# Moving a 30-column copy to ScalarE, merging four scans, and taking a rate ahead of a product, in a stick-breaking attention and convolution layer

## Chip, cores and metric

The kernel runs on one core of one Trainium2 chip. The metric is the device time of one execution in microseconds. The engines of the core are TensorE (PE in the profile, with its weight loads as PEld), VectorE (DVE), ScalarE (ACT), GpSimd (POOL) and SyncE (SP, which here only issues DMA transfers).

## The reference

One layer of a streaming encoder over 2048 tokens of width 1024, with 16 learned meta tokens in front. All arithmetic is in float32.

```python
u = rms_norm(h, pre_g)
glu_a, glu_b, conv_gate, q, k, v, sb_gate = split(u @ w_in)      # 7 x 512 columns

c = glu_a * sigmoid(glu_b)
c = causal_depthwise_conv(c, conv_w, conv_b)                     # 31 taps
c = silu(layer_norm(c)); c = (c @ w_pw2 + b_pw2) * silu(conv_gate)

# stick-breaking attention, 8 heads of 64: with z = q.k / 8 and s < t
# A[t,s] = sigmoid(z[t,s]) * prod over s < j < t of (1 - sigmoid(z[t,j]))
s = (A @ v) * silu(sb_gate)

mixed = concat([c, s]) @ w_out
out = (h + rms_norm(mixed, post_g))[16:]
```

## The kernel before, in words

**Number format.** Every float32 product is made of three products of a faster format: a value is split into a high part (a copy, by ScalarE) and a low part (the value less its high part, by VectorE or GpSimd). In the profile the names `uh` and `ul`, `ah` and `al`, and pairs called `w`, `mixs` or `mixc` are such parts.

**Chunks.** The tokens go through in four chunks of 512 (`c` = 0 to 3), each in four blocks of 128. Activations lie transposed, channels on the partitions. A chunk passes through these steps:

- *Projection*, `in_proj`: products of `uh`, `ul` with streamed weights into PSUM banks `mm`. `pairs` makes the gated convolution input: from the bank of `glu_b` ScalarE takes a sigmoid, and VectorE multiplies the bank of `glu_a` by it into `ct[j]`, one buffer for each of four groups of 128 channels (`j` = 0 to 3). `ct[j]` has 30 columns of history (`HIST`) ahead of the chunk's 512. For every chunk but the first, the last 30 columns of the chunk before are copied to the front of the buffer first: 12 copies in all (3 chunks, 4 groups). The product then overwrites the columns that the copy has read.
- *Convolution*: `conv` runs 31 taps on VectorE with the running sum in a PSUM bank `cv`; for some groups `conv_apart` makes each product on ScalarE (`pd`) and adds it on GpSimd (`acc`).
- *Attention*: for each head and key chunk, `weigh` makes logits in a PSUM bank `T`, ScalarE takes a sigmoid, and a scan on VectorE (`pr`) makes the running products. `flip` turns them on TensorE in another bank `T`, and splits the result: ScalarE writes `ah`, VectorE writes `al`, and the bank is free then. `gather` multiplies by the values (`vk`) into the bank `av`. There are four banks of `T`.
- *Meta tokens*, `meta_keys`: the same scan goes on over the 16 meta keys. `sgm` holds for each block and head 17 numbers, 16 sigmoids and a zero; `cm` holds zeros and, at the 17th place, the product that the head's scan ended with. Since `sgm` is zero there, the scan `max(state * sgm, cm)` starts afresh from that number at each head. For chunks 0, 1 and 2 all heads go together (`part` is false); for the last chunk they go in smaller parts.
- *Output*: `out_proj`, and for the last chunk `out_part` and `out_last`, with the norm over the mixed channels.

**Order.** One core's five engines each run their own list in order. The lists are written when the program is built, by a planner: `Clock` and `Engine` hold a model of what every instruction costs on its engine and when its inputs are there; `merge` picks, step by step, the next group of products of the attention stream (`main`), of the projections and the convolution (`fill`) and of the meta tokens (`extra`), and `step` issues the work of the other engines that is due by the model's clock of TensorE. Taps of the convolution are put into VectorE's gaps. So an instruction that is given to another engine changes the modelled clocks of both, and what is placed behind it can change with them. The code of the end, `out_last`, is written out by hand.

**The end.** The last chunk's last 256 columns are made last. `square` takes the sum of their squares on ScalarE (`accum_out`), VectorE multiplies them by the post-norm weights (`pg`), `rate` sums the partial sums on VectorE and takes the power -1/2 on GpSimd (`st`), and `give_out` multiplies by the rate, adds the input, on VectorE, and stores.

**The start.** `warm` issues transposes of the identity on TensorE while the first transfers are under way.

Every instruction is issued through one helper, so most rows of the profile name its line, L228; tiles and shapes tell the rows apart.

Of the kernel before, what the change touches and what calls it, by code (L numbers as in the profile page):

```python
# [14 lines left out]
AF = mybir.ActivationFunctionType  # L15
# [9 lines left out]
TC = 512  # L25
NCH = SEQ // TC
NTB = TC // P
# [5 lines left out]
HIST = CW - 1  # L33
# [243 lines left out]
def trunk(ctx: ExitStack, tc: tile.TileContext, x, xturn, xlater, meta, cpack, post_g, wpack, out):  # L277
# [20 lines left out]
    dve = Engine(clock, nc.vector, dve_cost, 0.04, run)  # L298
    act = Engine(clock, nc.scalar, act_cost, 0.04, run)
# [32 lines left out]
    def PT(tag, shape):  # L332
        bufs = BANKS[tag]
        room(tag, bufs)
        t = ps.tile(shape, F32, tag=tag, name=tag, bufs=bufs)
        clock.take(tag, bufs, t.name)
        return t
# [58 lines left out]
    ct = [const.tile([P, HIST + TC], F32, name=f"ct{j}") for j in range(NJ)]  # L396
# [151 lines left out]
    there = set()  # L548
# [226 lines left out]
    def warm():  # L775


        pt = PT("T", [P, TC])
        for _ in range(17):
            pe.transpose(pt[:, :P], ident, ident)  # L780

    waiting = []
# [8 lines left out]
    def tok():  # L791
        return T("tok", [P, 2, D], 2)
# [162 lines left out]
    def pairs(c, js):  # L955
        base = HIST - NM
        for j in js:
            sgb = []

            def ev_b(pt, o, n, j=j, sgb=sgb):  # L960
                if not sgb:
                    sgb.append(T("ehl", [P, NM + TC], EHL))
                t = sgb[0][:, o : o + n]

                def go():
                    dve.tensor_tensor(t, pt, row[:, o : o + n], op=ALU.mult)
                    act.activation(t, t, AF.Sigmoid)
                    if j < EARLY_PAIRS:

                        pool.tensor_tensor(t, t, row[:, o : o + n], op=ALU.mult)  # L970

                if c == 0 and j < EARLY_PAIRS:
                    with_rates(go)
                else:
                    act.activation(t, pt, AF.Sigmoid)

            def ev_a(pt, o, n, j=j, sgb=sgb):
                t, to = sgb[0][:, o : o + n], ct[j][:, base + o : base + o + n]

                def go():  # L980
                    dve.tensor_tensor(to, pt, t, op=ALU.mult)
                    if o + n < NM + TC:
                        return
                    if c and c - 1 not in parted:
                        parted_later.append(conv(c, j))
                    elif j in APART[c]:
                        taps_apart.append(conv_apart(c, j))
                    else:
                        taps.append(conv(c, j))

                if c == 0:
                    with_rates(go)
                else:
                    dve.tensor_copy(ct[j][:, 0:HIST], ct[j][:, TC : TC + HIST])
                    go()

            yield from proj(c, G_B + j, ev_b, True)
            if j < BEFORE[c]:
                yield need(given=lambda: j in accs[c - 1])
            yield from proj(c, G_A + j, ev_a, True)  # L1000
# [498 lines left out]
    def meta_keys(c, h0, h1, mixs):  # L1499

        hs = slice(h0, h1)
        part = h1 - h0 < NH
        yield need(
            given=lambda: all(("total", c, h) in keep for h in range(h1))
            and (c < NCH - 1 or ("conv" if h0 else "room", c) in keep)
        )
        for j in range(NJ):
            force(f"v{j}")
        bm = ev()[:, :TC].rearrange("p (b h s) -> p b h s", b=NTB, h=NH)
        hold.add(bm.name)  # L1510
        if part:
            pool.memset(bm, 0.0)
        sgm = sgms[c % 2]
        zm = sgm[:, :, hs, 0:NM]
        for r in range(NTB):
            fl = lambda t: t[:, r, hs].rearrange("p h s -> p (h s)")[:, ::-1]
            dve.tensor_tensor_scan(
                fl(sgm), fl(sgm), fl(cm), 0.0, op0=ALU.mult, op1=ALU.max
            )
        when(lambda: pool.tensor_copy(bm[:, :, hs], zm), [sgm], [bm])  # L1520
        given = {}
        force("s")
        force("g")

        def bring(j):
            sp.dma_start(given[j][1], sscr[c, j])
            sp.dma_start(given[j][0], gscr[c, j])
            when(lambda: rest(j), [given[j][1], vcol[c % 2]], [given[j][1]])

        def rest(j):  # L1530
            sr = given[j][1]
            s4 = sr.rearrange("p (b t) -> p b t", t=P)
            pool.tensor_tensor(
                s4, s4, vcol[c % 2][:, j].unsqueeze(2).to_broadcast([P, NTB, P]), op=ALU.add
            )

        def fetch(j):
            if j:
                given[j] = [ev()[:, :TC] for _ in range(2)]
                hold.update(t.name for t in given[j])  # L1540
            else:
                given[j] = keep["first given"]
            bring(j)

        js = range(h0 // 2, h1 // 2)
        if not part:
            both = [tok().rearrange("p j (i t) -> p j i t", i=2) for _ in range(2)]
            for j in js:
                given[j] = [both[j // 2][:, j % 2, i] for i in range(2)]
                in_us(0.8 * j, lambda j=j: bring(j), outs=[given[j][1]])  # L1550
        else:
            fetch(js[0])
        yield need(bm, tag="T", given=None if part else room_for_turned)
        hold.remove(bm.name)
        pt = PT("T", [P, TC])
        for r in range(NTB):
            pe.transpose(
                pt[:, r * P : (r + 1) * P], bm[:, r].rearrange("p h s -> p (h s)"), ident
            )
        high, low = slice(2 * NM, 4 * NM), slice(0, 2 * NM)  # L1560
        meets = {}
        turned = pt if part else T("ehl", [P, TC], EHL)
        if not part:
            act.activation(turned, pt, AF.Copy)
        for j in js:
            src = turned[2 * j * NM : 2 * (j + 1) * NM]
            m = meets[j] = T(*(("ehl", [P, TC], EHL) if part else ("mixs", [P, TC], 8)), F32R)
            hold.add(m.name)
            act.activation(m[high], src, AF.Copy)
            dve.tensor_tensor(m[low], src, m[high].bitcast(F32), op=ALU.subtract)  # L1570
            pool.tensor_copy(m[4 * NM : 6 * NM], m[high].bitcast(F32))
        if part:
            yield need(given=lambda: ("conv", c) in keep)
        for j in js:
            if j + 1 in js and j + 1 not in given:
                fetch(j + 1)
            gt, sr = given[j]
            m = meets[j]
            ready, t0 = need(m, vm, sr, gt, tag="T"), pe.now + 1.8
            yield lambda: ready() if part else max(ready(), t0)  # L1580
            pj = PT("T", [P, TC])
            pe.matmul(pj, vm[: 6 * NM, j], m[: 6 * NM], start=True, stop=True)
            hold.difference_update((sr.name, gt.name, m.name))
            dve.tensor_tensor(pj if part else sr, pj, sr, op=ALU.add)
            (dve if part else pool).tensor_tensor(sr, pj if part else sr, gt, op=ALU.mult)
            hi = T("mixs", [P, TC], 8, F32R)
            lo = T("mixs", [P, TC], 8, F32R)
            split(sr, hi, lo)
            mixs[j] = hi, lo
# [84 lines left out]
    def out_last(y, mh, ml):  # L1674
# [24 lines left out]
        def square(tb, src, n):  # L1699
            junk = T("ev", [P, TC], EV, BF16)[:, : src.shape[1]]  # L1700

            act.activation(
                junk, src, AF.Square, scale=D ** -0.5, accum_out=sums[:, tb, n : n + 1]
            )

        def place(tb, h):
            return y[tb // 2][:, tb % 2, h * TC : (h + 1) * TC]
# [5 lines left out]
            square(tb, a, 0)  # L1713
            dve.tensor_tensor(yt, a, pg[:, 0], op=ALU.mult)

        def add_second(tb, e=None, there=False):
            cols = slice(0, TC) if e is None else slice(e * OC, (e + 1) * OC)
            o = keep["o", tb, e or 0][:, cols]
            keep["end", tb, 1] = o if there else place(tb, 1)
            square(tb, o, 1 + (e or 0))  # L1720
            dve.tensor_tensor(o if there else place(tb, 1)[:, cols], o, pg[:, 1, cols], op=ALU.mult)

        def rate(tb):
            ss, rates[tb] = T("ss", [P, 1], 2), T("st2", [P, 1], 8)
            dve.tensor_reduce(ss, sums[:, tb], axis=mybir.AxisListType.X, op=ALU.add)
            pool.tensor_tensor(rates[tb], ss, nhalf, op=ALU.pow)
# [49 lines left out]
        finish_off(rest)  # L1776
        second(3, 1)
        give_out(2)
        add_second(3, 1)
        rate(3)  # L1780
        give_out(3)

    def out_proj(c, mixc, mixs):
# [262 lines left out]
```

## Time and profile before

| | |
|---|---|
| three runs | 1300.95, 1301.02, 1302.16 us (median 1301.02) |
| the profiled execution | 1302.12 us, of which its span from the first to the last instruction 1300.3 us |
| mean granted clock of TensorE | 0.997 |
| history copies on VectorE (128x30) | 12, together 8.6 us |
| meta scans on VectorE (128x136) | 12, together 7.4 us |
| warming transposes | 17, from 1.82 us on, 3.7 us |
| last product of TensorE begins at | 1293.5 us |

A row of a timeline has the start in us from the span's start, the duration, the engine, the helper's line, the operation, output and inputs (`ct<-mm,ehl` writes `ct` from `mm` and `ehl`), shapes, and how many instructions are merged in it; in brackets stands the time that the engine was idle before it and whose work ended that. A row of groups has the count, then the busy time in us and the mean in ns. A row of windows has the stretch, its length, the busy time of PE, PEld, DVE, ACT and POOL, the granted clock, the share of the DMA engines and GB/s.

### The profile page before, as it was taken

The numbers are of one execution on the slowest core, as the hardware profiler recorded it, in microseconds if no ns is written. First come the engines' busy times: TensorE is split into PE (matmuls) and PEld (weight loads), VectorE is DVE, ScalarE is ACT, GpSimd is POOL, SyncE is SP. The second block draws the span as 40 slices with busy tenths as digits, with TensorE's granted clock in tenths as the row PEclk, the third lists the DMA queues.
The fourth block names the chain that finished last, engine by engine and source line by source line (L and its number), as shares of the span: only waits on it lengthen the run. The fifth ranks groups of instructions, "written<-read, shape, count | busy, mean of one in ns | idle before, by whom it ended". The sixth has DMA issues, their size and how long they took to land. (4 is left out here: it accounts for less than half of the span.)

```text
span 1300.3 us, 22358 instructions
## 1 busy us (share of the span) xinstructions
PE 1280.6 (98%) x7458; PEld 1108.8 (85%) x7458; DVE 1022.3 (79%) x1426; ACT 792.1 (61%) x1666; POOL 694.5 (53%) x819
## 2 busy tenths in 40 slices
PE   8999998999999999999999999999999999999998
PEld 8998877888889988888889988888887899988897
DVE  5999898888986488984477569895558888898974
ACT  6544455444556555687755446688887865665653
POOL 2556567767687631586982242287788812132402
PEclk9999998999999999999999999999999999999999
DMA  6687875687977996676866697657667556587745
GB/s 241 217 266 250 271 234 178 211 249 239 291 242 245 311 327 188 193 241 200 283 209 181 176 313 239 177 169 231 215 207 228 158 150 188 172 263 235 232 138 182
DMA packets 177731, 290.57 MB, mean 223 GB/s; under 512 B 20928, under 2 KB 75392, under 8 KB 177616
## 3 DMA queue, kind: packets, MB, share of 16 engines
q1 hardware_dynamic: 166384, 251.65, 62.5%
q0 software_dynamic: 11232, 37.49, 7.6%
q8 instruction: 59, 0.97, 0.3%
q14 instruction: 56, 0.46, 0.1%
HBM read 222.10 MB, written 66.98 MB: 222 GB/s over the span
## 5 line engine op out<-in xcount | busy, mean ns | idle before, releaser
L228 PE MATMUL mm<-uh,w 128*128 128x512 f32 (+1 forms) x1936 | 562.5, 376 | 1.4 <-ACT uh L228 1.4
L228 PEld LDWEIGHTS mm<-uh,w 128*128 128x128 f32 x1936 | 337.5, 188 | 53.1 <-ACT uh L228 1.9
L228 PE MATMUL mm<-ul,w 128*128 128x512 f32 (+1 forms) x968 | 357.7, 371 | 1.3 <-DVE ul L228 1.3
L228 DVE TENSOR_TENSOR_SCAN pr<-T,pr,zcol 128x512 f32<-128x512 f32 x192 | 245.0, 1277 | 42.2 <-ACT T L228 40.4
L228 DVE TENSOR_TENSOR al<-T,ah 128x512 fp32r<-128x512 f32 (+1 forms) x320 | 192.1, 601 | 103.2 <-ACT ah L228 101.4
L228 ACT ACTIVATE ah<-T 128x512 fp32r<-128x512 f32 (+1 forms) x320 | 169.7, 530 | 127.5 <-PE T L228 126.3
L228 DVE SCALAR_TENSOR_TENSOR cv<-ct,cp,cv 128x512 f32<-128x512 f32 x319 | 239.1, 750 | 6.7
L228 POOL TENSOR_TENSOR acc<-acc,pd 128x512 f32<-128x512 f32 x150 | 193.7, 1291 | 56.4 <-ACT pd L228 50.2
L228 PEld LDWEIGHTS mm<-ul,w 128*128 128x128 f32 x968 | 181.7, 188 | 35.4 <-DVE ul L228 2.5
L228 POOL TENSOR_TENSOR w<-wr,w 128x512 fp32r<-128x512 f32 x132 | 171.0, 1298 | 74.9 <-ACT w L228 62.4
L228 PE MATMUL T<-kk,q 128*128 128x512 f32 (+4 forms) x704 | 201.2, 374 | 5.5 <-DVE al L228 4.9
L228 ACT ACTIVATE T<-T 128x512 f32<-128x512 f32 (+2 forms) x320 | 167.0, 523 | 50.2 <-PE T L228 43.5
L228 ACT ACTIVATE w<-wr 128x512 fp32r<-128x512 f32 x220 | 138.0, 628 | 95.9 <-PE mm L228 57.6
L228 PE MATMUL T<-ident,pr 128*128 128x128 f32 x1088 | 171.1, 272 | 0.6 <-DVE al L228 0.6
L228 PEld LDWEIGHTS T<-ident,pr 128*128 128x128 f32 x1088 | 133.9, 140 | 29.8 <-DVE al L228 1.0
L228 DVE TENSOR_TENSOR_SCAN pr<-T,tri 128x128 f32<-128x128 f32 (+3 forms) x128 | 104.3, 818 | 37.4 <-ACT T L228 33.9
L228 PEld LDWEIGHTS T<-kk,q 128*128 128x128 f32 x704 | 115.2, 190 | 21.0 <-DVE al L228 5.8
L228 PE MATMUL av<-al,vk 128*128 128x512 f32 (+1 forms) x320 | 117.2, 366 | 0.0
L228 PE MATMUL av<-ah,vk 128*128 128x512 f32 (+1 forms) x320 | 117.0, 366 | 0.0
L228 ACT ACTIVATE pd<-ct,cp 128x512 f32<-128x512 f32 x150 | 105.3, 714 | 1.4 <-POOL acc L228 1.2
L228 POOL COPY cm<-pr 128x1 f32<-128x1 f32 x120 | 24.8, 208 | 130.9 <-DVE pr L228 128.6
L228 PE MATMUL mm<-w,mixc 128*128 128x256 f32 x600 | 81.2, 284 | 0.0
(207 smaller groups left out, 1584.4 us busy)
## 6 DMA issues: line engine op xcount, KB each, us to landing
wr<-wpack SPq DMA_DIRECT2D x220, 256.0 KB, 3.8
w<-wscr SPq DMA_DIRECT2D x70, 512.0 KB, 4.6
vk<-vscr SPq DMA_DIRECT2D x80, 256.0 KB, 3.5
w<-lscr SPq DMA_DIRECT2D x80, 256.0 KB, 2.8
kk<-kscr SPq DMA_DIRECT2D x72, 256.0 KB, 4.3
q<-qscr SPq DMA_DIRECT2D x64, 256.0 KB, 5.3
wscr<-w POOLq DMA_DIRECT2D x28, 512.0 KB, 4.3
lscr<-w POOLq DMA_DIRECT2D x40, 256.0 KB, 3.5
```

The lines of the kernel that those rows point to most:

```text
L228: return call(out, *args, **kw)
```

## The change

Four edits. The history copy in `pairs` becomes an activation (plain copy) on ScalarE. In `meta_keys`, where all heads go together, one scan over all four blocks, 544 columns, replaces four of 136; in the last chunk's parts the four scans stay. In `out_last`, for the very last columns the rate is asked for between the square and the product: VectorE's sum comes ahead of its product, and GpSimd's power follows that sum. `warm` issues 22 transposes in place of 17.

```diff
         pt = PT("T", [P, TC])
-        for _ in range(17):
+        for _ in range(22):
             pe.transpose(pt[:, :P], ident, ident)
...
                 else:
-                    dve.tensor_copy(ct[j][:, 0:HIST], ct[j][:, TC : TC + HIST])
+                    act.activation(ct[j][:, 0:HIST], ct[j][:, TC : TC + HIST], AF.Copy)
                     go()
...
-        for r in range(NTB):
-            fl = lambda t: t[:, r, hs].rearrange("p h s -> p (h s)")[:, ::-1]
+        for rs in [slice(r, r + 1) for r in range(NTB)] if part else [slice(0, NTB)]:
+            fl = lambda t: (
+                t[:, rs.start, hs].rearrange("p h s -> p (h s)")
+                if part
+                else t.rearrange("p b h s -> p (b h s)")
+            )[:, ::-1]
             dve.tensor_tensor_scan(
                 fl(sgm), fl(sgm), fl(cm), 0.0, op0=ALU.mult, op1=ALU.max
             )
...
-        def add_second(tb, e=None, there=False):
+        def add_second(tb, e=None, there=False, rated=False):
             cols = slice(0, TC) if e is None else slice(e * OC, (e + 1) * OC)
             o = keep["o", tb, e or 0][:, cols]
             keep["end", tb, 1] = o if there else place(tb, 1)
             square(tb, o, 1 + (e or 0))
+            if rated:
+                rate(tb)
             dve.tensor_tensor(o if there else place(tb, 1)[:, cols], o, pg[:, 1, cols], op=ALU.mult)
...
         give_out(2)
-        add_second(3, 1)
-        rate(3)
+        add_second(3, 1, rated=True)
         give_out(3)
```

## The prediction

> **What bounds the kernel now.** I read the page first, for the busy shares and the granted clock.
>
> ```profile
> span 1300.3 us, 22358 instructions
> PE 1280.6 (98%) x7458; PEld 1108.8 (85%) x7458; DVE 1022.3 (79%) x1426; ACT 792.1 (61%) x1666; POOL 694.5 (53%) x819
> PEclk9999998999999999999999999999999999999999
> ```
>
> TensorE is busy for 1280.6 of 1300.3 us, and the diff removes no product of it. So all that can be won is the 19.7 us in which it is idle, and time in which its clock was cut: the clock row has one 8, the seventh slice of 32.5 us (195 to 228 us). Second, the waits of TensorE (us in total, times, longest).
>
> ```profile
> PE T L228 <- DVE al L228: 5.4, 4, 4.3
> PE T L228 <- DVE pr L228: 0.5, 2, 0.3
> ```
>
> One wait of 4.3 us stands out, for VectorE's `al` (the low half of turned weights, which frees a PSUM bank). Third, the timeline around it: VectorE, TensorE, GpSimd (start, duration, engine, work; idle before in brackets).
>
> ```profile
> 215.04 5.19 DVE L228 COPY ct<-ct 128x30 f32<-128x30 f32 x1
> 220.34 0.69 DVE L228 TENSOR_TENSOR ct<-mm,ehl 128x512 f32<-128x512 f32 x1
> 220.95 0.75 DVE L228 SCALAR_TENSOR_TENSOR cv<-ct,cp,cv 128x512 f32<-128x512 f32 x1
> 221.60 0.68 DVE L228 TENSOR_TENSOR al<-T,ah 128x512 fp32r<-128x512 f32 x1
> ...
> 217.74 0.26 PE L228 MATMUL T<-kk,q 128*128 128x16 f32 x1
> 222.34 1.43 PE L228 MATMUL T<-kk,q 128*128 128x512 f32 x3 [4.34 <-DVE al L228]
> ...
> 215.11 1.30 POOL L228 TENSOR_TENSOR w<-wr,w 128x512 fp32r<-128x512 f32 x1
> 216.36 2.50 POOL L228 TENSOR_TENSOR mixs<-acc,mixs 128x512 fp32r<-128x512 f32 x2
> 218.80 0.18 POOL L228 COPY cm<-pr 128x1 f32<-128x1 f32 x1
> 218.94 1.25 POOL L228 TENSOR_TENSOR w<-wr,w 128x512 fp32r<-128x512 f32 x1
> ```
>
> A copy of 30 columns, the history copy that the change moves, holds VectorE for 5.19 us. It ends at 220.23, when GpSimd's unbroken run of SBUF work ends (218.94 + 1.25 = 220.19). The `al` behind it comes out at 222.28, and TensorE, idle since 218.00, goes on at 222.34. Fourth, the granted clock by stretches (after the length: busy us of PE, PEld, DVE, ACT, POOL; then the clock).
>
> ```profile
> 217.99:220.25 2.26, 0.01 (x1) 0.00 (x0) 2.25 (x1) 0.56 (x2) 2.26 (x4) 1.00 0.00 0
> 220.25:222.34 2.09, 0.00 (x0) 0.00 (x0) 2.00 (x4) 0.00 (x0) 0.47 (x1) 0.50 0.52 210
> 222.34:227.07 4.73, 4.73 (x13) 3.86 (x14) 4.07 (x6) 2.22 (x5) 1.54 (x4) 0.50 0.40 129
> ```
>
> The idle time also cost clock: it fell to 0.50 at 220.25 and stayed there until 227.07. TensorE worked 4.73 us of that at half speed, so 4.73 / 2 = 2.4 us more are lost. The stall costs 4.34 + 2.4 = 6.7 us.
>
> **The change part by part.**
>
> *History copies to ScalarE.* Twelve copies leave VectorE.
>
> ```profile
> L228 DVE COPY ct<-ct x12: 156/174/5194, 200.3 to 869.1; 128x30 f32<-128x30 f32 x12
> L228 DVE SCALAR_TENSOR_TENSOR cv<-ct,cp,cv x319: 722/756/757, 32.6 to 876.0; 128x512 f32<-128x512 f32 x160
> 852.05 0.82 DVE L228 COPY ct<-ct 128x30 f32<-128x30 f32 x1
> 869.13 0.90 DVE L228 COPY ct<-ct 128x30 f32<-128x30 f32 x1
> 850.00:875.00 25.00, 25.00 (x126) 20.70 (x125) 23.18 (x29) 21.72 (x40) 21.69 (x22) 1.00 0.46 150
> ```
>
> Their sum is 12 x 717 ns = 8.6 us of VectorE, which is not the bound; only the stall counts. Two others also outlasted a GpSimd instruction (0.82 and 0.90 us) and cost TensorE nothing: it was busy for all 25.00 us around them. So a hold of 0.9 us is covered, and 5.19 us was not. What would be late next: the product `ct<-mm,ehl`, a convolution tap `cv<-ct`, then `al`. The taps, with one operand in PSUM, never took over 757 ns in 319, GpSimd busy or not. Without the copy the product runs from 215.1, the tap from 215.8, and `al` from about 216.4 to 217.1, its `ah` being there at 216.30 (below): ahead of TensorE's need at 218.0. I take the whole 6.7 us. The other end: if TensorE met a wait of some 2.5 us there for another reason, 6.7 - 2.5 = 4.2 us would be left.
>
> On ScalarE no 30-column copy is shown. The nearest rows give a price:
>
> ```profile
> L228 ACT ACTIVATE sgm<-T 128x16 f32<-128x16 f32 x128 | 23.0, 180 | 32.3 <-PE T L228 31.9
> L228 ACT ACTIVATE T<-T 128x128 f32<-128x128 f32 x32 | 8.4, 262 | 1.0
> 214.26 0.62 ACT L228 ACTIVATE mixs<-acc 128x512 fp32r<-128x512 f32 x1
> 215.70 0.60 ACT L228 ACTIVATE ah<-T 128x512 fp32r<-128x512 f32 x1
> sum 12.00, PE 12.00 PEld 9.72 DVE 10.66 ACT 4.40 POOL 5.87; mean PE 1.00 PEld 0.81 DVE 0.89 ACT 0.37 POOL 0.49
> ```
>
> 16 columns take 180 ns and 128 take 262, so 30 take about 190 ns by the line between; twelve add 2.3 us to an engine that idles 39% of the span. A wait is added: VectorE's product, which overwrites the copied columns, now waits for ScalarE, and queued behind it on VectorE stand taps, `al` and scans, for which TensorE waits. The last row sums twelve windows, the microsecond before each copy: ScalarE is busy 4.40 of 12.00 us there. At the stall it ends `mixs` at 214.88, so the copy ends near 215.1 and the product loses nothing. Bounds for one copy: from a 0.2 us gain (VectorE is rid of 174 ns) to the rival below; I take 0, because a hold under 0.9 us was covered.
>
> *The order.* The program's order comes from a planner with costs of its own, and the copy's cost moves from VectorE's clock to ScalarE's. From the first copy at 200 us on, taps and transfers may be placed a step earlier or later. Beside the big stall TensorE's waits after 200 us are small (5.4 - 4.3 = 1.1 us for `al`, 0.5 for `pr`), so there is little to win. I take 0, with -1 to +3 for the range; the upper end is a wait of the next size, half of the worst one with no cut in the clock.
>
> *One scan for four blocks.* At three places four scans of 136 columns become one of 544.
>
> ```profile
> 343.39 2.48 DVE L228 TENSOR_TENSOR_SCAN sgm<-sgm,cm 128x136 f32<-128x136 f32 x4
> L228 DVE TENSOR_TENSOR_SCAN pr<-T,pr,zcol 128x512 f32<-128x512 f32 x192 | 245.0, 1277 | 42.2 <-ACT T L228 40.4 <-POOL ev L228 0.6
> ```
>
> Four took 2.48 us; one of 544 takes about 1277 x 544 / 512 = 1.36 us, so VectorE wins 1.1 us a place, or nothing if GpSimd holds it once. At most the 0.5 us that TensorE waits for scans is in reach. I take 0 (-0.5 to +0.3).
>
> *Five more warming transposes.*
>
> ```profile
> 1.82 3.71 PE L228 MATMUL T<-ident 128*128 128x128 f32 x17 [1.82 <-POOL ident masks.py:199]
> 6.91 0.75 PE L228 MATMUL mm<-uh,w 128*128 128x264 f32 x4 [1.38 <-ACT uh L228]
> ```
>
> At 3.71 / 17 = 0.22 us each, five take 1.1 us, within the 1.38 us in which TensorE waits for its first operand. The cover left is 0.3 us; were the operand earlier, up to 1.1 us would show. The clock is in full in the first slices, so nothing is won either: 0.
>
> *The last rate ahead of the last product.*
>
> ```profile
> 1294.43 0.19 ACT L228 ACTIVATION_READ_ACCUMULATOR ev<-cv 128x1 f32 x1
> 1294.65 0.42 DVE L228 TENSOR_TENSOR tok<-cv,uh 128x256 f32<-128x256 f32 x1
> 1294.99 0.15 DVE L228 TENSOR_REDUCE ss<-sq 128x1 f32<-128x4 f32 x1
> 1295.22 0.55 POOL L228 TENSOR_TENSOR st<-ss,nhalf 128x1 f32<-128x1 f32 x1 [0.79 <-DVE ss L228]
> 1295.81 1.42 DVE L228 SCALAR_TENSOR_TENSOR ul<-tok,st,ul 128x512 f32<-128x512 f32 x2 [0.67 <-POOL st L228]
> ```
>
> The product already waits for ScalarE's square, so nothing is lost if the sum goes first. It starts at 1294.65 in place of 1294.99; GpSimd's power follows 0.34 us sooner, and the product (0.42 us) fits beside its 0.55 us. The two last operations and the stores behind them move by 0.34 us: -0.3, with 0 as the other end.
>
> **Sum.** -6.7 - 0.3 = -7.0 us. The profiled execution took 1302.12 us (span 1300.3 and 1.8 around it), which gives 1295.1. It is 1.1 us above the median of the three runs; from that, 1301.02, the sum gives 1294.0. I forecast the middle, 1294.5.
>
> **Rivals.**
>
> *The clock is not lost in every run.* The cut came 2.26 us after TensorE stopped, and a run's gap of 4.3 us might also end before it. Then only 4.34 + 0.3 = 4.6 us come back: 1296.4. For it: the three runs differ by 1.2 us. Against: all lie near the profiled time. The Trainium skill ("TensorE: Matmul & The Clock Gate", part 1) says that the window of about 3.4 us that decides runs free, whenever work begins. By that rule a gap of 4.3 us holds a whole idle window only in some runs, and this rival would stand; the trace's 6.8 us at half clock (220.25 to 227.07) agree with two such windows, its cut after 2.26 us of idle does not agree with a whole one.
>
> *Another stall takes its place.* Replanned, some VectorE instruction with both reads in SBUF can fall beside a dense run of GpSimd. These rows show that it happens:
>
> ```profile
> 187.51 4.15 DVE L228 SCALAR_TENSOR_TENSOR ul<-tok,cp,uh 128x512 fp32r<-128x512 f32 x2
> PE mm L228 <- DVE ul L228: 1.3, 1, 1.3
> ```
>
> That pair took 4.15 us and cost TensorE 1.3. A stall like the one removed would give all back: 1301. Against it: in 1300 us there is one such. The Trainium skill ("SBUF — State Buffer", section "SBUF: two separate sides") says that VectorE and GpSimd lock a shared port pair, and that whoever begins first keeps it for that instruction. By that a hold would last one GpSimd instruction, about 1.3 us, and this rival would cost almost nothing; the 5.19 us over five instructions contradict it, so I keep it.
>
> *ScalarE's queue holds the product (slower).* If the copy stands behind a ScalarE instruction that itself waits for TensorE, VectorE stands still.
>
> ```profile
> ACT ah L228 <- PE T L228: 126.3, 136, 3.1
> ```
>
> Such waits reach 3.1 us; less the covered 0.9, a copy would cost up to 2.2 us. It decides from about five of twelve: 5 x 2.2 = 11, less 7.0, is 4 us slower, 1305. Against it: the idle ScalarE before the copies.
>
> *The change does not do what it says:* VectorE is held beside GpSimd by the next instruction too, and only the tail is won, 1300.7. The taps' 757 ns speak against it.
>
> **Numbers.** Forecast 0.72; clock not lost in every run 0.06; another stall 0.12; ScalarE's queue 0.07; no effect 0.03. The measurement tells about 0.2% (2.6 us) from no change, that is, 1298.4 to 1303.6. Faster: 0.72 + 0.06 = 0.78; same: 0.12 + 0.03 = 0.15; slower: 0.07. The range runs from 1294.0 less 2 us (order and scans better) to 1300.5, which takes in the clock's rival and half-sized new stalls.
>
> **What would show it.** Right: no VectorE hold near 215 us; no wait of TensorE for `al` over 1 us after 200 us; the clock row without its 8; history copies on ScalarE near 0.2 us; 0.3 us less from the last product to the end. Wrong: a new idle stretch of TensorE over 2 us with a cut of the clock, or `ct<-mm,ehl` waiting for ScalarE for over 1 us.

## The result and the profile after

The changed kernel took 1294.30 us (median of four runs, 1294.10 to 1294.78), beside 1301.59 us (1300.95 to 1302.63) for the kernel before on the same chip. The ratio is 0.9944, with a 95% interval of 0.9927 to 0.9961: faster by 0.56%, and within 0.2 us of the forecast, 1294.5 us.

The page of the changed kernel: the span, the engines' busy time, and TensorE's granted clock in forty slices.

```profile
span 1292.5 us, 22357 instructions
PE 1278.8 (99%) x7463; PEld 1108.3 (86%) x7463; DVE 1011.7 (78%) x1405; ACT 793.3 (61%) x1678; POOL 695.4 (54%) x819
PEclk9999999999999999999999999999999999999999
```

The two pages give the whole balance. The span fell by 7.8 us. TensorE's busy time fell by 1.8 us although it has five transposes more, which is work at half clock that is gone; its idle time fell from 19.7 to 13.7 us, by 6.0. The clock row has lost its 8. VectorE has 10.6 us less to do, which by itself buys nothing: it was never the bound.

TensorE's longest waits after the change (us in total, times, longest).

```profile
PE T L228 <- DVE al L228: 1.3, 2, 1.1
PE mm L228 <- DVE ul L228: 1.3, 1, 1.3
PE T L228 <- DVE ul L228: 1.2, 2, 0.7
PE av L228 <- POOL rate L228: 1.0, 1, 1.0
PE T L228 <- DVE pr L228: 0.2, 1, 0.2
```

The 4.3 us for `al` are gone. The 1.1 us for `al` that is now the longest of its row lies at 983 us. The 1.3 us for `ul` were there before the change.

The timeline of the changed kernel at the place of the stall: ScalarE, VectorE, GpSimd.

```profile
214.23 0.22 ACT L228 ACTIVATE ct<-ct 128x30 f32<-128x30 f32 x1
...
214.49 0.68 DVE L228 TENSOR_TENSOR ct<-mm,ehl 128x512 f32<-128x512 f32 x1
215.09 0.74 DVE L228 SCALAR_TENSOR_TENSOR cv<-ct,cp,cv 128x512 f32<-128x512 f32 x1
215.77 0.69 DVE L228 TENSOR_TENSOR al<-T,ah 128x512 fp32r<-128x512 f32 x1
...
214.55 1.30 POOL L228 TENSOR_TENSOR w<-wr,w 128x512 fp32r<-128x512 f32 x1
215.81 2.54 POOL L228 TENSOR_TENSOR mixs<-acc,mixs 128x512 fp32r<-128x512 f32 x2
218.30 0.17 POOL L228 COPY cm<-pr 128x1 f32<-128x1 f32 x1
218.44 1.29 POOL L228 TENSOR_TENSOR w<-wr,w 128x512 fp32r<-128x512 f32 x1
```

GpSimd does the same unbroken work as before, and VectorE's product, tap and `al` run beside it at their usual length, as the prediction had them (`al` ends at 216.46, some 0.6 us before the time that it gave). The windows of the same two stretches in which TensorE was idle or at half speed before (after the length: busy PE, PEld, DVE, ACT, POOL; then the clock).

```profile
217.99:222.34 4.35, 4.35 (x21) 3.57 (x20) 3.67 (x5) 3.00 (x7) 4.35 (x8) 1.00 0.64 224
222.34:227.07 4.73, 4.73 (x22) 3.79 (x21) 3.83 (x6) 2.54 (x4) 4.42 (x6) 1.00 0.84 273
```

TensorE is busy throughout at the full clock. In 222.34 to 227.07 it does 22 products where the kernel before did 13.

### The profile page after: what moved, and what is told of

The parts are those of the page before. It is cut to its first block, busy times and chain, and to the rows that moved or that the text cites. A ratio compares the mean times of both kernels' runs of the same rounds, so it can differ in the third digit from the quotient of the medians.

```text
span 1292.5 us, 22357 instructions
## 1 busy us (share of the span) xinstructions
PE 1278.8 (99%) x7463; PEld 1108.3 (86%) x7463; DVE 1011.7 (78%) x1405; ACT 793.3 (61%) x1678; POOL 695.4 (54%) x819
## 5 line engine op out<-in xcount | busy, mean ns | idle before, releaser
L228 PE MATMUL mm<-uh,w 128*128 128x512 f32 (+1 forms) x1936 | 562.4, 376 | 0.0
L228 PEld LDWEIGHTS mm<-uh,w 128*128 128x128 f32 x1936 | 337.5, 188 | 51.7 <-ACT uh L228 0.4
L228 PE MATMUL mm<-ul,w 128*128 128x512 f32 (+1 forms) x968 | 357.7, 371 | 1.3 <-DVE ul L228 1.3
L228 DVE TENSOR_TENSOR_SCAN pr<-T,pr,zcol 128x512 f32<-128x512 f32 x192 | 244.9, 1276 | 43.1 <-ACT T L228 41.0
L228 DVE TENSOR_TENSOR al<-T,ah 128x512 fp32r<-128x512 f32 (+1 forms) x320 | 191.9, 600 | 106.2 <-ACT ah L228 104.0
L228 ACT ACTIVATE ah<-T 128x512 fp32r<-128x512 f32 (+1 forms) x320 | 169.7, 530 | 127.4 <-PE T L228 126.1
L228 DVE SCALAR_TENSOR_TENSOR cv<-ct,cp,cv 128x512 f32<-128x512 f32 x319 | 239.0, 749 | 6.7
L228 POOL TENSOR_TENSOR acc<-acc,pd 128x512 f32<-128x512 f32 x150 | 193.6, 1291 | 56.4 <-ACT pd L228 51.0
L228 PEld LDWEIGHTS mm<-ul,w 128*128 128x128 f32 x968 | 181.7, 188 | 35.3 <-DVE ul L228 2.5
L228 POOL TENSOR_TENSOR w<-wr,w 128x512 fp32r<-128x512 f32 x132 | 172.3, 1307 | 72.7 <-ACT w L228 60.6
L228 PE MATMUL T<-kk,q 128*128 128x512 f32 (+4 forms) x704 | 200.4, 373 | 0.5 <-DVE al L228 0.2
L228 ACT ACTIVATE T<-T 128x512 f32<-128x512 f32 (+2 forms) x320 | 167.0, 523 | 49.2 <-PE T L228 42.4
L228 ACT ACTIVATE w<-wr 128x512 fp32r<-128x512 f32 x220 | 138.0, 628 | 92.2 <-PE mm L228 43.2
L228 PE MATMUL T<-ident,pr 128*128 128x128 f32 x1088 | 171.0, 272 | 1.1 <-DVE al L228 1.1
L228 PEld LDWEIGHTS T<-ident,pr 128*128 128x128 f32 x1088 | 134.0, 140 | 30.1 <-DVE al L228 1.6
L228 DVE TENSOR_TENSOR_SCAN pr<-T,tri 128x128 f32<-128x128 f32 (+3 forms) x128 | 104.3, 818 | 37.3 <-ACT T L228 33.7
L228 PEld LDWEIGHTS T<-kk,q 128*128 128x128 f32 x704 | 114.8, 189 | 15.4 <-DVE pr L228 0.9
L228 PE MATMUL av<-al,vk 128*128 128x512 f32 (+1 forms) x320 | 117.0, 366 | 0.0
L228 PE MATMUL av<-ah,vk 128*128 128x512 f32 (+1 forms) x320 | 116.9, 365 | 0.0
L228 ACT ACTIVATE pd<-ct,cp 128x512 f32<-128x512 f32 x150 | 105.4, 714 | 1.4 <-POOL acc L228 1.2
L228 POOL COPY cm<-pr 128x1 f32<-128x1 f32 x120 | 25.2, 212 | 127.8 <-DVE pr L228 123.3
L228 PE MATMUL mm<-w,mixc 128*128 128x256 f32 x600 | 81.1, 284 | 0.0
```

The costliest lines, as they stand in the source:

```text
L228: return call(out, *args, **kw)
```

## Experiments

Ratios are to the kernel before on the same chip, whose medians were 1301.25 to 1302.29 us. Some kernels below write a spare tile that nothing reads; no other result changes. In kernels in which the edit shifts the helper, its rows name L229 in place of L228, and L301, L479, L998 and L1209 are lines of the edits.

### Which edit brings the gain

*The copy alone*: the kernel before, in its own order, with only the copies issued on ScalarE.

```diff
...
+    dve.other["tensor_copy"] = lambda out, src: nc.scalar.activation(out, src, AF.Copy)
```

> The kernel before with its order kept, and only the twelve history copies issued on ScalarE (four scans, old tail, 17 transposes stay). Theory 1, the copy held beside GpSimd's unbroken run is the whole stall: no TensorE wait over 1 us near 215 us, the clock not cut, 6.7 us less than before, about 1294.9 us. Theory 2, the stall comes only in part from the copy (VectorE late anyway, or the other three edits share the gain): a wait for al of 2 us or more stays, 1297 to 1300 us.

Measured: 1295.40 us (1294.56 to 1296.87), ratio 0.9952 [0.9937, 0.9967]. No wait of TensorE near 215 us is left; its waits for `al` are down to 0.8 us in all. The copy alone carries nearly the whole gain. Its profiled execution had a cut of the clock near the start all the same (8.25 to 11.66 us); it is taken up under *The clock* below.

*The copies back*: the changed kernel with its twelve copies issued on VectorE, everything else and the order of all instructions as changed.

```diff
...
-                    act.activation(ct[j][:, 0:HIST], ct[j][:, TC : TC + HIST], AF.Copy)
+                    act.history(ct[j][:, 0:HIST], ct[j][:, TC : TC + HIST], AF.Copy)
...
+    act.other["history"] = lambda out, src, f: nc.vector.tensor_copy(out, src)
```

> The changed kernel with its order kept, and only the twelve history copies issued on VectorE again. Theory 1: one copy near 214.5 us takes about 5 us, TensorE idles over 4 us, the clock falls to 0.5 for about 7 us, about 1301 us. Theory 2: the wait is shorter, under 1298 us.

Measured: 1300.98 us (1300.29 to 1303.46), 0.9996 [0.9986, 1.0005]: the gain is gone. The timeline (VectorE, TensorE) and the windows of this kernel.

```profile
214.84 5.19 DVE L301 COPY ct<-ct 128x30 f32<-128x30 f32 x1
222.14 0.85 PE L229 MATMUL T<-kk,q 128*128 128x512 f32 x3 [4.34 <-DVE al L229]
```

```profile
217.80:222.14 4.34, 0.00 (x0) 0.00 (x0) 4.24 (x5) 0.55 (x2) 2.72 (x4) 1.00 0.25 102
222.14:222.95 0.81, 0.81 (x5) 0.72 (x6) 0.78 (x2) 0.18 (x1) 0.00 (x0) 1.00 0.26 101
222.95:226.37 3.42, 3.42 (x11) 2.75 (x10) 3.42 (x5) 2.21 (x4) 1.04 (x4) 0.50 0.47 101
```

The hold and the idle time are those of before to the hundredth of a microsecond. The cut of the clock is not: 3.42 us at half speed here, which costs 1.7 us, beside 6.82 us before, of which TensorE worked 4.73 us and lost 2.4.

*Seventeen warming transposes* in place of 22, *four scans* in place of one, and the *old tail* (the last sum after the product), each in the changed kernel otherwise unedited.

```diff
-        for _ in range(22):
+        for _ in range(17):
```

> The changed kernel with 17 warming transposes in place of 22. My step (they cost and win nothing): the time of the changed kernel, 1294.3 us within 0.3. Rival: the first product at 6.57 us in place of 6.91, and all until 191 us 0.5 us sooner, came of the five transposes: 1294.8 us and a first product at 6.9 us.

```diff
-        for rs in [slice(r, r + 1) for r in range(NTB)] if part else [slice(0, NTB)]:
+        for rs in [slice(r, r + 1) for r in range(NTB)]:
...
-                if part
+                if True
```

> The changed kernel with four scans of 136 in place of one of 544 at the three places. My step (off TensorE's path): 1294.3 us within 0.5, VectorE 1.1 us later at each place, one of each four scans near 1.47 us. Rival (scans are on the path): 0.3 to 1.5 us slower, with a TensorE wait for al or pr behind each place.

```diff
-        add_second(3, 1, rated=True)
+        add_second(3, 1)
+        rate(3)
```

> The changed kernel with the last rate behind the last product again. My step: from the start of TensorE's last product to the start of VectorE's last operation 2.70 us in place of 2.41, and the time 0.3 us longer, 1294.6 us. Rival (the last store's landing sets the end and takes the gain): the 0.3 us shows on VectorE and not in the span, 1294.3 us.

Measured: seventeen transposes 1293.91 us (1293.41 to 1296.34), 0.9943 [0.9924, 0.9963]; four scans 1294.87 us (1294.37 to 1296.93), 0.9950 [0.9934, 0.9965]; old tail 1294.66 us (1293.52 to 1295.26), 0.9940 [0.9927, 0.9953]. None differs from the changed kernel by more than its runs scatter. For the tail, the profile says why. The last VectorE operations with their waits, first of the old tail, then of the changed kernel:

```profile
1286.00 0.52 PE L228 MATMUL cv<-acc,mixs 128*128 128x256 f32 x3
1288.33 1.42 DVE L228 SCALAR_TENSOR_TENSOR ul<-tok,st,ul 128x512 f32<-128x512 f32 x2 [0.66 <-POOL st L228]
```

```profile
1285.56 0.52 PE L228 MATMUL cv<-acc,mixs 128*128 128x256 f32 x3
1287.55 1.41 DVE L228 SCALAR_TENSOR_TENSOR ul<-tok,st,ul 128x512 f32<-128x512 f32 x2 [0.33 <-POOL st L228]
```

From TensorE's last group to VectorE's last operations it is 2.33 us with the old tail and 1.99 us with the new: 0.34 us won, as forecast. But the spans, 1292.9 and 1292.5 us, end 6.9 us after the last group in both (1292.9 - 1286.00 and 1292.5 - 1285.56). What lies between is the transfer of the last five stores, 256 KB each. The windows of these transfers, first of the old tail, then of the changed kernel (share of the DMA engines and GB/s at the end of the row):

```profile
1287.70:1291.00 3.30, 0.00 (x0) 0.00 (x0) 1.42 (x2) 0.00 (x0) 0.55 (x1) 1.00 0.94 351
```

```profile
1287.30:1290.50 3.20, 0.00 (x0) 0.00 (x0) 1.41 (x2) 0.00 (x0) 0.21 (x1) 0.91 0.96 360
```

In both kernels the DMA engines are nearly full for over 3 us there. Asking 0.34 us sooner for the last two of the five stores does not move the end of transfers that are already one behind another.

### Which instructions are held

The theory was that VectorE needs for a copy with both ends in SBUF something that GpSimd's run of SBUF work keeps. To vary the instruction with everything else kept, one spare instruction of 30 columns went ahead of the product in the changed kernel, at the place of the stalling copy: a copy from SBUF, a copy from PSUM, and an addition of two SBUF operands.

```diff
...
+                    if c == 1 and j == 1:
+                        nc.vector.tensor_copy(spare[:, 0:HIST], spare[:, HIST:])    # from SBUF
+                        nc.vector.tensor_copy(spare[:, 0:HIST], pt[:, 0:HIST])      # or: from PSUM
+                        nc.vector.tensor_tensor(spare[:, 0:HIST], spare[:, HIST:],  # or: two inputs
+                                                tri[:, 0:HIST], op=ALU.add)
```

> The changed kernel with one more VectorE instruction at one place, ahead of the convolution product of chunk 1, group 1 (near 214.5 us): a 30-column copy from SBUF to SBUF between spare columns. Its result is not used. Theory 1 (a copy with both ends in SBUF is held while GpSimd runs unbroken): it takes about 5 us and brings the whole stall back, about 1301 us. Theory 2 (any VectorE instruction there would wait, or only the real copy's data do): 0.2 us, 1294.5 us.

> As the kernel with the spare copy, but the 30 columns are read from the product's PSUM bank. Theory 1: not held, 0.2 us, 1294.5 us. Rival (any VectorE write to SBUF is held beside GpSimd): 5 us, 1301 us.

> As the kernel with the spare copy, but the added instruction is an addition of 30 columns with both inputs in SBUF. Theory 1a (two SBUF reads are held as a copy is, as the 3.49 us of ul suggest): about 5 us, 1301 us. Theory 1b (only a copy from SBUF to SBUF is held until a break, two reads only until the end of one GpSimd instruction): at most 1.3 us, 1294.3 to 1295 us.

The spare instruction in the three timelines, in this order:

```profile
215.27 5.22 DVE L998 COPY spare<-spare 128x30 f32<-128x30 f32 x1
```

```profile
214.45 0.16 DVE L998 COPY spare<-mm 128x30 f32<-128x30 f32 x1
```

```profile
215.17 5.20 DVE L998 TENSOR_TENSOR spare<-spare,tri 128x30 f32<-128x30 f32 x1
```

The times: 1301.19 us, 0.9994 [0.9985, 1.0003], from SBUF; 1294.56 us, 0.9947 [0.9930, 0.9964], from PSUM; 1301.46 us, 0.9996 [0.9987, 1.0005], with two inputs. In each of the three, GpSimd's first `w` of the stretch begins 0.06 to 0.07 us after the spare instruction. One instruction of 30 columns puts the whole gain back, and the same instruction with its source in PSUM costs nothing that can be measured. So the hold comes from where the operands lie, not from the real copy's data or its place in the order. That two inputs are held no less refutes the version of the theory by which only copies are.

### What ends the hold

In the kernel before the hold ended with GpSimd's stretch. Two candidates coincide there: GpSimd's first instruction that is not SBUF arithmetic (a DMA issue, without idle time before it), and the first point at which GpSimd cannot go on: the instruction behind that DMA waits 3.95 us for VectorE's `pr`, which itself stands behind the held copy. Both kernels here are "the copies back" with one small DMA that GpSimd issues within the stretch. In the first it reads a spare tile and waits for nothing; in the second it reads the `mixs` just written, so that GpSimd waits for its own result.

```diff
...
-            split(accs[j], hi, lo)
+            pause = lambda: nc.gpsimd.dma_start(spare_out, spare)                 # waits for nothing
+            pause = lambda lo=lo: nc.gpsimd.dma_start(                            # or: waits for its own lo
+                spare_out, lo[:, 0 : 2 * HIST].bitcast(F32))
+            split(accs[j], hi, lo, then=pause if (c, j) == (0, 2) else None)
```

> The kernel with the twelve copies back on VectorE, and GpSimd's run broken once: after the low part of group 2 of chunk 0's convolution (near 217.1 us) it issues a small transfer of spare columns to a spare place in HBM. Theory 1 (the hold lasts until GpSimd's first break): the copy ends near 217.2 us, 2.6 us long, TensorE idles about 1.7 us, the clock is not cut, about 1296 us. Rival (the hold lasts a set time, or until the copy of cm or the transfer that followed): about 5 us, 1301 us or more.

> As the kernel with the pause, but the small transfer reads 60 columns of the low part that GpSimd has just written, so that GpSimd waits for its own result before it goes on. The pause without such a wait lengthened the hold (5.78 us) and did not end it. New theory 1b (the hold lasts until GpSimd waits for a result of its own, or runs out of work): the copy ends near 217.3 us, 2.6 us long, TensorE idles about 1.7 us, the clock is not cut, about 1296 us. Rival (only the end of the whole run frees it): 5.8 us again, 1301 us.

The timeline with the DMA that waits for nothing (VectorE, GpSimd):

```profile
214.64 5.78 DVE L301 COPY ct<-ct 128x30 f32<-128x30 f32 x1
...
217.18 0.57 POOL L1209 DMA_DIRECT2D spare_out<-spare  x1
217.78 1.27 POOL L229 TENSOR_TENSOR mixs<-acc,mixs 128x512 fp32r<-128x512 f32 x1
...
219.12 1.26 POOL L229 TENSOR_TENSOR w<-wr,w 128x512 fp32r<-128x512 f32 x1
220.32 0.55 POOL L229 DMA_DIRECT2D wscr<-w  x1
224.86 0.18 POOL L229 COPY cm<-pr 128x1 f32<-128x1 f32 x1 [3.98 <-DVE pr L229]
```

And with the DMA that waits (VectorE, GpSimd, TensorE):

```profile
215.36 2.65 DVE L301 COPY ct<-ct 128x30 f32<-128x30 f32 x1
...
216.66 1.30 POOL L229 TENSOR_TENSOR mixs<-acc,mixs 128x512 fp32r<-128x512 f32 x1
218.26 0.57 POOL L1209 DMA_DIRECT2D spare_out<-mixs  x1 [0.29 <-POOL mixs L229]
...
220.12 0.84 PE L229 MATMUL T<-kk,q 128*128 128x512 f32 x3 [1.80 <-DVE al L229]
```

The first time is 1301.24 us, 0.9995 [0.9986, 1.0005]; the second 1297.02 us, 0.9960 [0.9944, 0.9976]. A DMA without a wait does not release VectorE; the hold is only longer, by about the 0.57 us of that DMA, at 5.78 us, and ends again with the last `w` (219.12 + 1.26 = 220.38; the copy ends at 220.42). The DMA behind that `w` starts without idle time; what GpSimd then waits for, 3.98 us, is VectorE's `pr` and not a result of its own. My first reading, a hold until GpSimd's first break, fell. With the wait, the copy ends at 218.01, right behind the `mixs` that ends at 217.96, while GpSimd waits for it; TensorE then idles 1.80 us, with no cut of the clock. Both kernels fit one reading: the hold lasts at the longest until GpSimd has to wait, for itself or for another engine. None of the VectorE holds in the fourteen profiles goes on through idle time of GpSimd.

A wait is not needed every time, though. In the changed kernel a scan of 16 columns, which took 0.22 us at 1214.20 us, is held to 1.21 us soon after (VectorE, GpSimd):

```profile
1215.94 1.21 DVE L228 TENSOR_TENSOR_SCAN uh<-sgm,pr,zcol 128x16 f32<-128x16 f32 x1
...
1215.80 2.54 POOL L228 TENSOR_TENSOR acc<-ev,acc 128x512 fp32r<-128x512 f32 x2
```

It ends at 1217.15 us, about where the first of GpSimd's two additions ends, and these run on to 1218.34 without idle time. What decides whether GpSimd's next instruction goes ahead of a held one of VectorE is not shown.

The other cure follows: leave the arithmetic and break GpSimd's runs. In the changed kernel GpSimd copies one column of each low part that it has just split (181 of them) into a spare column, which makes it wait for itself.

```diff
...
             eng.tensor_tensor(lo, y, hi.bitcast(F32), op=ALU.subtract)
+            if eng is pool:
+                nc.gpsimd.tensor_copy(spare, lo[:, 0:1].bitcast(F32))
```

> The changed kernel, with a copy of one column on GpSimd behind each of its 181 low parts, which waits for that low part. Theory 1b: no VectorE hold lasts over about one GpSimd instruction; ul near 187 us takes 2.2 us or less in place of 3.48, TensorE's idle 1.25 us near 190.5 us goes, about 1293 us. Rival (181 x 0.2 = 36 us more of GpSimd make low parts late, TensorE waits for weights): 1295 us or more.

Measured: 1291.71 us (1291.39 to 1292.15), 0.9918 [0.9905, 0.9931]. It was timed beside the old tail on one chip, five runs each, and no run of either lies among the other's. GpSimd is busy 728.8 us in place of 695.4, and the median of the kernel is the lowest of all. The pair of `ul` near 187 us shows where half of the gain comes from; first the changed kernel, then this one (VectorE, GpSimd):

```profile
186.98 4.15 DVE L228 SCALAR_TENSOR_TENSOR ul<-tok,cp,uh 128x512 fp32r<-128x512 f32 x2
187.38 2.52 POOL L228 TENSOR_TENSOR w<-wr,w 128x512 fp32r<-128x512 f32 x2
```

```profile
186.30 2.80 DVE L228 SCALAR_TENSOR_TENSOR ul<-tok,cp,uh 128x512 fp32r<-128x512 f32 x2
186.58 1.30 POOL L228 TENSOR_TENSOR w<-wr,w 128x512 fp32r<-128x512 f32 x1
187.94 0.54 POOL L477 COPY spare<-w 128x1 f32<-128x1 f32 x1
188.44 1.82 POOL L228 TENSOR_TENSOR w<-wr,w 128x512 fp32r<-128x512 f32 x1
```

The pair takes 2.80 us in place of 4.15, and the 1.3 us that TensorE waited for `ul` behind it are gone. With 0.7 us less waiting for `ul` near 52 us, that is 2.0 of the 2.6 us between 1294.3 and 1291.7. Now GpSimd is the one that waits: its copy takes 0.54 us and its next `w` 1.82 us, where 0.18 and 1.30 are usual.

Last, both: the copies on VectorE again, with GpSimd's waits for itself.

> The changed kernel with its twelve history copies issued on VectorE again and, behind each low part that GpSimd splits, a copy of one column of that result into a spare column, so that GpSimd waits for a result of its own about every two instructions. The engines' other instructions and their order stay. Theory (VectorE's copy is held until GpSimd waits for a result of its own): no copy is held for more than about 2.7 us, the one near 214 us for 1.3 to 2.7 us; TensorE loses at most 1.8 us there with no cut of the clock, and the time is about 1292 to 1293.5, some 0 to 2 us above the changed kernel with the waits and the copies on ScalarE (1291.7). Rival (the copy is held until GpSimd's stretch of work ends, whatever waits lie within it): a hold of 5 us or more near 214 us, TensorE idle for 4 us or more with the clock cut, and about 1298.5, which is 1291.7 and the 6.7 us of the stall.

Measured: 1292.16 us (1291.21 to 1293.79), 0.9932 [0.9915, 0.9949]. The group of the copies, and the longest hold among the twelve with what GpSimd did:

```profile
L301 DVE COPY ct<-ct x12: 156/173/1555, 197.3 to 858.2; 128x30 f32<-128x30 f32 x12
```

```profile
254.27 1.55 DVE L301 COPY ct<-ct 128x30 f32<-128x30 f32 x1
...
254.48 1.30 POOL L229 TENSOR_TENSOR w<-wr,w 128x512 fp32r<-128x512 f32 x1
255.84 0.18 POOL L479 COPY spare<-w 128x1 f32<-128x1 f32 x1
```

The longest hold is 1.55 us and ends (255.82) as GpSimd's `w` does (255.78), ahead of its wait for itself. Moving the copies to ScalarE was one cure, then, and not the only one. The expectation put a hold of 1.3 to 2.7 us near 214 us; the copy there began at 212.00 instead, between two GpSimd instructions, and took 0.16 us. So this kernel does not test a hold at that place again; the DMA that waits does.

## Why the prediction was right

*The stall* (6.7 us of the sum of 7.0). Shown in both directions: the copy alone takes it away, the copies back bring it back, and so does one foreign SBUF instruction at the same place, but not one from PSUM. The prediction let the hold end with GpSimd's unbroken run, and for this stretch that was so. As a reason it was too coarse: a DMA can break the run without effect, and a wait of GpSimd for its own result ends the hold in the middle of it. The prediction's two other long copies fit the later reading: 0.82 and 0.90 us, each ending with an addition into `acc` behind which GpSimd idles for ScalarE's `pd`, 0.56 and 0.65 us.

*The clock* (2.4 us of the 6.7). Its size was right for the profiled execution but is no constant: 1.7 us with the copies back (3.42 / 2), 2.8 us with the spare copy from SBUF, where the cut held from 221.19 to 228.01 and TensorE worked 5.62 us of it. The rival "the clock is not lost in every run" is thus true in part: the loss came in every profile with a stall of over 4 us, in two sizes. In four of these five profiles the cut began 0.9 to 2.1 us before TensorE went on, and lasted 6.82 us; with the copies back it began 0.81 us after, and lasted 3.42 us. A long stall is not the only way to such a loss: in the profile of the copy alone, TensorE idled 1.83 us ahead of its first product at 7.18 us, and its clock was 0.50 from 8.25 to 11.66 us, which cost 1.7 us there. The Trainium skill ("TensorE: Matmul & The Clock Gate", part 1) has windows of about 3.4 us that run free; cuts of 3.42 and 6.82 us agree with one and two of these. That a whole idle window must pass first does not agree: the cut came 2.26 us after TensorE stopped in the kernel before.

*"ScalarE's queue holds the product."* It did not. The copy on ScalarE, as a group of the changed kernel:

```profile
L228 ACT ACTIVATE ct<-ct 128x30 f32<-128x30 f32 x12 | 2.6, 219 | 0.0
L228 DVE TENSOR_TENSOR_SCAN sgm<-sgm,cm 128x544 f32<-128x544 f32 x3 | 3.8, 1270 | 0.0
```

219 ns each, beside the 190 ns that the line through 16 and 128 columns gave: 0.4 us off over twelve, on an engine with time to spare.

*"Another stall takes its place."* It did not, but the stall named for it, the pair of `ul`, stayed, with its 1.3 us. The Trainium skill ("SBUF — State Buffer", section "SBUF: two separate sides") says that VectorE and GpSimd lock a shared port pair for one instruction. Which VectorE instructions it names agrees with the three spare instructions (two SBUF inputs held, PSUM source not); the duration does not: 5.2 us span five GpSimd instructions. The runs show when these holds end, not what holds VectorE.

*The order* (0, -1 to +3). The doubt was empty: but for the edits, every engine's list holds the same instructions in the same order in both kernels. Giving the copy to another engine moved nothing else in the plan.

*One scan* (0). 1.27 us beside the estimated 1.36; VectorE wins 1.2 us at three places, and four scans cost no measurable time. The size was right, but one sign that the prediction named, no wait for `al` over 1 us after 200 us, did not hold. The wait at 983 us comes with the single scan; first the changed kernel, then the one with four scans:

```profile
983.09 0.44 PE L228 MATMUL T<-ident,pr 128*128 128x128 f32 x2 [1.14 <-DVE al L228]
```

```profile
985.63 0.44 PE L228 MATMUL T<-ident,pr 128*128 128x128 f32 x2 [0.59 <-DVE al L228]
```

Against the 0.55 us stands a wait of 0.27 us for `pr`, 6 us earlier, in the kernel with four scans, which the changed kernel no longer has.

*Warming transposes* (0). Right in size: seventeen make no measurable difference in time. The start won 0.3 us all the same (first product at 6.57 in place of 6.91), and not from the transposes: with seventeen of them it began at 6.59. The first operand came earlier in that execution; over the profiles the first product came between 6.4 and 7.2 us. Whether five more transposes keep the clock from a cut like that of the copy alone, which had seventeen, is not shown.

*The tail* (-0.3). This is the term that was mis-sized. VectorE's last operations did move by 0.34 us against TensorE, but the span ends with the landing of the last stores, whose transfers fill the DMA engines, and nothing was won: from the end of the last product to the end of the span it is 6.3 us before and 6.4 after, where the prediction named 0.3 us less as a sign. In its place stands the start's 0.3 us, and some 0.5 us of TensorE's busy time that I cannot assign: it fell by 1.8 us, where 2.4 less for the clock and 1.1 more for five transposes make 1.3. That the total came within 0.2 us of the forecast is therefore in part luck.

## What to carry to other kernels

When a tiny VectorE instruction with all its operands in SBUF shows several microseconds, look at GpSimd's row beside it: the duration is not its work but that of the GpSimd instructions beside it, at the longest up to the next point at which GpSimd waits, for a result of its own or for another engine. Either read from PSUM or move the instruction to ScalarE, or break GpSimd's stretch with a cheap instruction that depends on the one before. Price such a stall by what TensorE waits for behind it, and add the clock that the idle time costs as a range, not as a number.

## What was not expected of the hardware

- A VectorE hold beside GpSimd outlives five GpSimd instructions (5.19 us) and a DMA issue that waits for nothing (5.78 us), and ends in the middle of GpSimd's stretch at a wait of GpSimd for itself (2.65 us).
- An added wait can make a kernel faster: 181 copies of one column on GpSimd, 33 us of its time, took the kernel from 1294.3 to 1291.7 us.
- The cut of the clock after an idle time of 4.2 to 4.9 us lasted 3.42 or 6.82 us. After an idle time of 1.80 us at 220 us there was none; after one of 1.83 us at the start, in the profile of the copy alone, there was one of 3.41 us.
